# A hybrid mixer trunk on one core: S5's VectorE work is put behind four splits and modulation tiles, and two in-projections move around a norm

## The chip, the cores and the metric

The kernel runs on one core of a Trainium2 chip. The metric is the device time of one execution in microseconds (us). Engines: PE is TensorE's matmul, PEld its weight load, DVE is VectorE, ACT is ScalarE, POOL is GpSimd, and SP is the queue that issues most DMAs. Each engine takes its own instructions strictly in the order in which the program was laid out; between engines there are semaphores.

## The reference, cut to what matters

One layer, 1024 tokens, width 1024, float32:

```python
mod = silu(c) @ w_ada + b_ada                     # 6 x 1024 modulation values
sh1, sc1, g1, sh2, sc2, g2 = split(mod, 6)
h = x * (1 + sc1) + sh1
z = h @ w_in + b_in                               # 14 tiles of 128 columns
z_h, z_b, z_c, z_p, z_cv, z_cg, z_s = split(z, 7)
y_a = z_b * causal_dwconv(z_c * z_h, sc_w)        # short convolution
y_b = pool_mixer(z_p)                             # trailing means
y_c = silu(layer_norm(causal_dwconv(z_cv * sigmoid(z_cg), 31 taps)))   # conformer
y_d = ssm_mixer(z_s)                              # S5: complex diagonal state, then a GLU
y = concat(y_a, y_b, y_c, y_d) @ w_o
x = layer_norm(ALPHA * x + (1 + g1) * y)
x = layer_norm(ALPHA * x + (1 + g2) * ffn(x * (1 + sc2) + sh2))
```

## The kernel before

A float32 matmul is made of three passes (`passes`, L129 to L132) over operands that were cut into a high and a low part. `split` (L80, L81) makes the parts: ACT casts the high one, DVE subtracts to get the low one. `pair` does this for a weight tile of 128x1024 into one of two rotating buffers, `pr0` and `pr1`. Weights come in through `raw` (L73): one SP DMA into one of four rotating 512 KB buffers.

One modulation tile is `ada(j)` (L166): a `raw` load, a DVE multiply with a running sum (L168, 128x1024) and a small DVE add (L170). There are 48.

The order of the stages: a first loop over eight k tiles (L192) does `ada(8+k)`, `ada(k)`, makes `h` for both 512-token halves (ACT L205, splits to `h_a` and `h_b`) and accumulates four of the in-projections (`GRP_A`) in all eight PSUM banks. The last DVE instruction of `ada(7)` is kept as `gate`. Then comes S5's preparation (`SSM.weights`, L1138): a long chain of small operations on 8 to 32 columns, on POOL, from the decay constants to their powers, and from L1216 on operations on 128 and 512 columns on DVE, which multiply those results into four tables; PE transposes them (L1259) and makes kernels (L1270, L1271). Each of those DVE operations is ordered behind `gate`:

```python
i = e.tensor_tensor(out=o, in0=a, in1=b, op=op)
if self.gate is not None and not self.pool:
    self.after(i, self.gate)
```

`SSM.run` (L1302) is the scan itself; its last DMA writes `yg_d` (L1357). The memory of S5 is then given to the pool `yp` (y0 to y7, two more weight pairs `prb`, rows). The first writes into `yp` wait for that last DMA of S5.

Meanwhile PE works through the ten remaining in-projections, `REST` = 11, 9, 4, 0, 5, 1, 6, 7, 2, 3, each one weight pair and two halves (`half`, 24 matmuls each). 11 and 9 feed the conformer's convolution (31 taps on two channel tiles, L429, on DVE). `h_b` is needed up to the last half of projection 3; its memory then takes `ys`, the split operands of the output projection.

The order of DVE, ACT, POOL and SP is laid out by the framework's scheduler from its own costs, by priority of the program's order. In the block from L868 on PE's order is that of the program (`in_order(ON_PE)`). There: the conformer norm's transposes (`run(conf, 2)`: PE L445, DVE statistics L449 and L451, a POOL chain of 14 operations for the reciprocal root, ACT L457), pooling, the two halves of projection 7, then `ada(16)` to `ada(23)`, the norm's second transposes (L463), pooling's matmul (L380), S5's GLU (`ssm_glu`, L294) with the halves of projection 2 between its two parts, projection 3, and the output projection, whose row of gates `g1row` needs `ada(16)` to `ada(23)` and is spread by a DMA of 1024 single values (`spread`, L470).

Of the kernel before, what the change touches and what calls it, by code (L numbers as in the profile page):

```python
# [9 lines left out]
F32 = mybir.dt.float32  # L10
# [4 lines left out]
ADD, SUB, MUL = ALU.add, ALU.subtract, ALU.mult  # L15
# [6 lines left out]
NCH = T // CH  # L22
# [5 lines left out]
TAU = 8  # L28
NS = T // TAU
WARM = 28  # L30
GU_FIRST = 7
CF = 5
T1, T2, T3 = 6, 2, 12
# [3 lines left out]
REST = (11, 9, 4, 0, 5, 1, 6, 7, 2, 3)  # L37
# [13 lines left out]
def trunk(ctx: ExitStack, tc: tile.TileContext, A, out):  # L51
    nc = tc.nc
    V, S, G, PE, SP = nc.vector, nc.scalar, nc.gpsimd, nc.tensor, nc.sync
# [14 lines left out]
    def sm():  # L68
        return ps.tile([P, 512], F32, name="sm", tag="sm", bufs=2)

    def raw(src, cols=1024):
        t = raw_p.tile([P, 1024], F32, name="raw", tag="raw", bufs=4)
        SP.dma_start(t[:, :cols], src)  # L73
        return t
# [3 lines left out]

    def split(hi, lo, src):
        S.copy(hi, src)  # L80
        V.tensor_tensor(out=lo, in0=src, in1=hi.bitcast(F32), op=SUB)  # L81

    def pair(src):
        pt = pair_tile()
        split(pt[:, 0], pt[:, 1], src)
        return pt
# [36 lines left out]
    def run(g, n=1000):  # L123
        for _ in range(n):
            if next(g, g) is g:
                break
# [39 lines left out]
    def ada(j):  # L166
        w = raw(A["w_ada"][j])
        V.scalar_tensor_tensor(out=w, in0=w, scalar=1.0, in1=cond, op0=MUL, op1=MUL,  # L168
                               accum_out=mod[:, j:j + 1])
        return V.tensor_tensor(out=mod[:, j:j + 1], in0=mod[:, j:j + 1], in1=bada[:, j:j + 1], op=ADD)  # L170
# [14 lines left out]
    wm = sm()  # L185
    for i in range(WARM):
        PE.matmul(wm[:, :128], ident, ident, start=True, stop=True)
# [3 lines left out]
            za[m, c] = mm() if m != 10 else sm()  # L191
    for k in range(KT):  # L192
        ada(8 + k)
        gate = ada(k)
        w_k = raw(A["w_inA"][k], 512)
        x_k = tmp()
        step = T if k else CH
        for c0 in range(0, T, step):
            SP.dma_start(x_k[:, c0:c0 + step], A["xT"][k][:, c0:c0 + step])
        wp = pair_tile()  # L200
        split(wp[:, 0, :512], wp[:, 1, :512], w_k[:, :512])
        for c in range(NCH):
            hh, hl = hk(c, k)
            xc = x_k[:, c * CH:(c + 1) * CH]
            S.activation(xc, xc, AF.Identity, scale=mod[:, 8 + k:9 + k], bias=mod[:, k:k + 1])  # L205
            split(hh, hl, xc)
        if k in (0, KT - 1):
            unpack("pack2" if k else "pack1")
        for c in range(NCH):
            for i, m in enumerate(GRP_A):  # L210
                ms = slice(i * P, (i + 1) * P)
                passes(za[m, c], (wp[:, 0, ms], wp[:, 1, ms]), hk(c, k), k == 0, k == KT - 1)
# [20 lines left out]
    def cs(c):  # L233
        return slice(c * CH, (c + 1) * CH)


    def glu_gate(i, zz):
        sg = tmp()
        for c in range(NCH):
            S.activation(sg[:, cs(c)], zz[c], AF.Sigmoid, bias=bin_[:, 10 + i:11 + i])  # L240
        return sg

    def glu_val(i, zz, sg):
        for c in range(NCH):
            V.scalar_tensor_tensor(out=up[i][:, TAPS - 1 + c * CH:TAPS - 1 + (c + 1) * CH], in0=zz[c],
                                   scalar=bin_[:, 8 + i:9 + i], in1=sg[:, cs(c)], op0=ADD, op1=MUL)

    ssm = SSM(tc, A, packs, sp, sm, ident, after)
    scr = {}
# [48 lines left out]
                        in1=sg.rearrange("p (t n) -> p t n", t=TAU), op=MUL)  # L298


    def w_in(m):
        return pair(raw(A["w_inB"][REST.index(m)]))

    def half(w, c):
        o = mm()
        for k in range(KT):
            ks = slice(k * P, (k + 1) * P)
            passes(o, (w[:, 0, ks], w[:, 1, ks]), hk(c, k), k == 0, k == KT - 1)
        return o

    def project(m):
        w = w_in(m)
        return [half(w, c) for c in range(NCH)]

    sg1 = glu_gate(1, project(11))
    glu_val(1, project(9), sg1)

    def short_in(i):
        zc = zch[i][:, 2:]
# [22 lines left out]
    def pool_in(i, c, zz):  # L342
        S.activation(zp[i][:, 16 + c * CH:16 + (c + 1) * CH], zz, AF.Identity, bias=bin_[:, 6 + i:7 + i])
# [4 lines left out]
    for i in range(2):  # L348
        for hf in range(2):
            w = 2 << (2 * i + hf)  # L350
# [35 lines left out]
    zz = project(6)  # L386
# [46 lines left out]
    def conformer(c, acc, bank):  # L433
        nt = tmp()
        st = cst.tile([P, 4, 6], F32, name="cst_", bufs=2)
        mv = cst.tile([P, 4, 2], F32, name="cmv", bufs=2)
        rs = cst.tile([P, 4], F32, name="crs", bufs=2)
        nb = cst.tile([P, 4], F32, name="cnb", bufs=2)
        tp = []
        for h in range(2):  # L440
            o = bank()
            for q in range(2):
                t = 2 * h + q
                for i in range(2):
                    PE.transpose(o[:, q * 256 + i * P:q * 256 + (i + 1) * P],  # L445
                                 acc[i][:, t * P:(t + 1) * P], ident)
            tp.append(o)
        for t in range(4):
            V.bn_stats(st[:, t], tp[t // 2][:, (t % 2) * 256:(t % 2) * 256 + 256])  # L449
        for t in range(4):  # L450
            V.bn_aggr(mv[:, t], st[:, t])  # L451
        rsqrt(rs, mv[:, :, 1])
        G.tensor_tensor(out=nb, in0=mv[:, :, 0], in1=rs, op=MUL)
        G.tensor_scalar(out=nb, in0=nb, scalar1=-1.0, scalar2=None, op0=MUL)
        yield
        for t in range(4):
            S.activation(nt[:, t * 256:(t + 1) * 256], tp[t // 2][:, (t % 2) * 256:(t % 2) * 256 + 256],  # L457
                         AF.Identity, scale=rs[:, t:t + 1], bias=nb[:, t:t + 1])
        yield
        for i in range(2):  # L460
            o = bank()
            for t in range(4):
                PE.transpose(o[:, t * P:(t + 1) * P], nt[:, t * 256 + i * P:t * 256 + (i + 1) * P], ident)  # L463
            S.activation(y[4 + i][:, cs(c)], o, AF.Silu, scale=cfg[:, i:i + 1], bias=cfb[:, i:i + 1])
# [402 lines left out]
    cnt[0] = 2  # L867
    with in_order(ON_PE):  # L868
        w, w2 = w_in(7), w_in(2)
        conf = conformer(0, acc, mm)  # L870
        run(conf, 2)
        fin0 = pooling(0, 0)
        for c in range(NCH):
            pool_in(1, c, half(w, c))
        w3 = w_in(3)
        for j in range(16, 24):
            ada(j)
        fin1 = pooling(1, 0)
        run(conf)
        fin0()  # L880
        ssm_glu(0)
        zz = [half(w2, 0)]
        ssm_glu(1)
        zz.append(half(w2, 1))
        short_out(0, zz)
        fin1()
        for n in range(2):
            wy.append(out_prep(n, K0[n]))
            ada(32 + n)
        acc, taps = conv(1)  # L890
        zz = [half(w3, c) for c in range(NCH)]
        g1row = spread(mod[:, 16:24], "rowa")
        for j in range(34, 40):
            ada(j)
        run(taps, T1)
        short_out(1, zz)

        for n in range(3):
            if n > 1:
                wy.append(out_prep(n, K0[n]))  # L900
            first_step(n)
            ada(24 + 2 * n)
            ada(25 + 2 * n)
            run(taps, T2)
        for j in range(30, 32):
            ada(j)
        for h in range(2):
            o0[3, h] = sm()
        for n in range(3):
            out_step(o0, wy[n][1], wy[n][0], 3, n == 0, False)  # L910
        wy = [out_prep(n, k) for n, k in zip((3, 4, 0, 1, 2), K1)]

        V.tensor_tensor(out=hA, in0=l1g, in1=mod[:, 32:40], op=MUL)
        V.tensor_tensor(out=hB, in0=l1b, in1=mod[:, 32:40], op=MUL)
        V.tensor_tensor(out=hB, in0=hB, in1=mod[:, 24:32], op=ADD)
        ln = []

        def tail(t, lo=0, hi=5):
            for n in range(lo, hi):
                out_step(o0, wy[n][1], wy[n][0], t, False, n == 4)  # L920

        def stats(t):
            rr.append(res1(0, t, o0))
            ln.append(ln1(0, t, rr[t], h2))
            run(ln[t], 1)
        tail(0)
        tail(1)
        tail(2, 0, 2)
# [44 lines left out]
    with tc.issue_after(ln_end[0]), tc.issue_after(ln_end[1]), in_order(ON_PE):  # L973
        for f in range(2, GU_FIRST):
            run(c11(f))
# [24 lines left out]
        def mid():  # L1000
            run(conf)
            spare = [sl.tile([P, 2, 1024], F32R, name="pr", tag=f"m_{n}") for n in ("up", "zch", "zp")]
            cc.extend([c11(GU_FIRST, spare[:2]), c11(GU_FIRST + 1, (spare[2], None))])
            cc.extend(c11(j) for j in range(GU_FIRST + 2, FT // 2))
            run(cc[0], 1)
# [420 lines left out]
```

## Time and profile before

| | |
|---|---|
| median of 3 runs | 1038.14 us (1037.73 to 1041.8) |
| the profiled execution, own time | 1037.87 us |
| its span, first to last instruction | 1036.1 us |
| mean granted TensorE clock | 0.980 |
| busy in the span | PE 980.8, DVE 737.7, ACT 344.5, POOL 184.4 us |

The span is 1.8 us shorter than the execution's own time. PE is busy 95% of the span, so the places where it waits are what the table cannot show and what has to be looked for along the time axis.

### The profile page before, as it was taken

Reading aid. Unit: us, or ns where it says so; the run is one execution under the profiler, and the core shown is the slowest. Engines: PE = TensorE matmul, PEld = TensorE weight load, DVE = VectorE, ACT = ScalarE, POOL = GpSimd, SP = SyncE. Lnnn points to the kernel's source line nnn. Section 1 sums busy time; section 2 is a strip of 40 time slices with the busy share of each in tenths; the row PEclk is TensorE's granted clock in tenths of the full one; section 3 lists DMA queues with packets and bytes.
Section 4 is the critical chain, followed back from the end, with each engine's and each line's share of the span. In section 5 each row is a group of like instructions: output and inputs, shape, how many; then the busy total and the mean of one; then the engine's idle time right before and its main releaser. Section 6 shows DMA issues by size and latency. Waiting matters only on the chain.

```text
span 1036.1 us, 12527 instructions
## 1 busy us (share of the span) xinstructions
PE 980.8 (95%) x4480; PEld 799.9 (77%) x4480; DVE 737.7 (71%) x1184; ACT 344.5 (33%) x537; POOL 184.4 (18%) x515
## 2 busy tenths in 40 slices
PE   8949999898989989899899999999999999999995
PEld 7837777676887868687688888887888888888884
DVE  5858998888669952757898777776568433776656
ACT  4632211424464351374322222222233333312500
POOL 7990000300351020541000000000000000050013
PEclk9979999998999999899999999999999999999998
DMA  8833212686454363597954344443247534654601
GB/s 314 321 112 104 53 41 90 219 225 223 158 204 172 147 237 104 188 316 267 347 175 159 138 147 152 146 148 111 82 149 284 174 136 142 232 185 148 228 21 61
DMA packets 65694, 177.75 MB, mean 172 GB/s; under 512 B 11040, under 2 KB 17216, under 8 KB 65632
## 3 DMA queue, kind: packets, MB, share of 16 engines
q1 hardware_dynamic: 57760, 149.17, 42.7%
q0 software_dynamic: 7872, 27.79, 6.7%
q8 instruction: 35, 0.57, 0.2%
q14 instruction: 27, 0.22, 0.1%
HBM read 142.26 MB, written 34.09 MB: 170 GB/s over the span
## 4 chain that ended last, share of the span: by engine, by line
PE 60%; DVE 10%; DMA 5%; POOL 4%; ACT 3%; issue 2%; SPq 0%; DVEq 0%; POOLq 0%; ACTq 0%
PE mm L132 18%; PE mm L130 18%; PE mm L131 17%; PE sm L130 2%; PE sm L132 2%; PE sm L131 2%; DMA raw<-in_w_ada_dram 2%; DMA raw<-h_d 2%; DVE pr L81 1%; DVE acc L429 1%; DMA raw<-in_w_gate_dram 1%; DVE raw L168 1%; ACT tmp L598 1%; DVE lst L500 1%; POOL rs_a L397 1%
## 5 line engine op out<-in xcount | busy, mean ns | idle before, releaser
L81 DVE TENSOR_TENSOR pr<-raw,pr 128x1024 fp32r<-128x1024 f32 (+1 forms) x139 | 138.1, 1003 | 77.7 <-ACT pr L80 77.4
L80 ACT CAST pr<-raw 128x1024 fp32r<-128x1024 f32 (+1 forms) x139 | 119.2, 878 | 179.4 <-PE sm L132 68.4
L130 PE MATMUL mm<-bop,pr 128*128 128x512 f32 x264 | 103.2, 391 | 4.2 <-DVE c L767 3.5
L131 PE MATMUL mm<-bop,pr 128*128 128x512 f32 x264 | 102.8, 389 | 0.0
L132 PE MATMUL mm<-bop,pr 128*128 128x512 f32 x264 | 102.7, 389 | 0.0
L130 PE MATMUL mm<-h,pr 128*128 128x512 f32 (+1 forms) x208 | 77.0, 370 | 8.0 <-ACT p L643 7.1
L429 DVE SCALAR_TENSOR_TENSOR acc<-up,pack,acc 128x512 f32<-128x512 f32 x120 | 84.3, 742 | 0.1
L130 PE MATMUL mm<-pr,acts 128*128 128x512 f32 x216 | 84.0, 389 | 0.0
L131 PE MATMUL mm<-pr,acts 128*128 128x512 f32 x216 | 84.0, 389 | 0.0
L132 PE MATMUL mm<-pr,acts 128*128 128x512 f32 x216 | 84.0, 389 | 0.0
L132 PE MATMUL mm<-h,pr 128*128 128x512 f32 (+1 forms) x208 | 75.4, 362 | 2.9 <-DVE pr L81 2.9
L131 PE MATMUL mm<-h,pr 128*128 128x512 f32 (+1 forms) x208 | 75.2, 361 | 0.0
L132 PE MATMUL mm<-tb,pr 128*128 128x512 f32 x176 | 68.8, 391 | 1.1 <-DVE pr L81 1.0
L130 PE MATMUL mm<-tb,pr 128*128 128x512 f32 x176 | 68.7, 390 | 1.0 <-ACT pr L80 1.0
L131 PE MATMUL mm<-tb,pr 128*128 128x512 f32 x176 | 68.5, 389 | 0.0
L397 POOL TENSOR_SCALAR rs_a<-lmv 128x1 f32<-128x1 f32 x16 | 11.0, 689 | 318.1 <-DVE lmv L503 317.8
L168 DVE SCALAR_TENSOR_TENSOR raw<-raw,cond 128x1024 f32<-128x1024 f32 x48 | 58.1, 1218 | 13.3 <-DMA raw<-in_w_ada_dram 13.2
L80 ACT CAST pr<-room 128x512 fp32r<-128x512 f32 x60 | 34.3, 619 | 87.9 <-PE mm L132 83.9
L130 PEld LDWEIGHTS mm<-bop,pr 128*128 128x128 f32 x264 | 49.6, 188 | 16.4 <-DVE c L767 2.9
L132 PEld LDWEIGHTS mm<-bop,pr 128*128 128x128 f32 x264 | 49.6, 188 | 10.3
L131 PEld LDWEIGHTS mm<-bop,pr 128*128 128x128 f32 x264 | 49.6, 188 | 10.1
L131 PE MATMUL mm<-h_a,pr 128*128 128x512 f32 x104 | 42.7, 410 | 13.7 <-DVE h_a L81 13.5
(311 smaller groups left out, 2182.4 us busy)
## 6 DMA issues: line engine op xcount, KB each, us to landing
raw<-in_w_ada_dram SPq DMA_DIRECT2D x48, 512.0 KB, 4.8
raw<-in_w_down_dram SPq DMA_DIRECT2D x44, 512.0 KB, 3.7
raw<-in_w_gate_dram SPq DMA_DIRECT2D x23, 512.0 KB, 4.7
raw<-in_w_up_dram SPq DMA_DIRECT2D x23, 512.0 KB, 4.2
raw<-act_d SPq DMA_DIRECT2D x44, 256.0 KB, 3.3
raw<-in_w_o_dram SPq DMA_DIRECT2D x16, 512.0 KB, 4.4
p_d<-p POOLq DMA_DIRECT2D x11, 512.0 KB, 2.9
act_d<-tmp POOLq DMA_DIRECT2D x11, 512.0 KB, 2.9
```

The lines of the kernel that those rows point to most:

```text
L80: S.copy(hi, src)
L81: V.tensor_tensor(out=lo, in0=src, in1=hi.bitcast(F32), op=SUB)
L130: PE.matmul(o, wh, xh, start=first, stop=False, skip_group_check=True)
L131: PE.matmul(o, wh, xl, start=False, stop=False, skip_group_check=True)
L132: PE.matmul(o, wl, xh, start=False, stop=last, skip_group_check=True)
L168: V.scalar_tensor_tensor(out=w, in0=w, scalar=1.0, in1=cond, op0=MUL, op1=MUL, accum_out=mod[:, j:j + 1])
L397: G.tensor_scalar(out=a, in0=v, scalar1=EPS, scalar2=None, op0=ADD)
L429: V.scalar_tensor_tensor(out=o, in0=u, scalar=dww[:, i, j:j + 1], in1=o, op0=MUL, op1=ADD)
L500: V.bn_stats(st[:, h], r[:, h * 512:(h + 1) * 512])
L598: S.activation(dst, src, AF.Identity, scale=hA[:, kk:kk + 1], bias=hB[:, kk:kk + 1])
```

## The change

`w_in` and the pairs of projections 11 and 9 are traced before S5's preparation, and so are `ada(16)` to `ada(19)`; `gate` becomes the last DVE instruction of `ada(19)`. In the later block the halves of projection 7 come before the norm's first transposes, `ada(20)` to `ada(23)` alone are left there, and both halves of projection 2 come between the norm's two sets of transposes. (`split` now returns its instruction; nothing uses it.)

```diff
+EARLY = 4
...
     for k in range(KT):
         ada(8 + k)
-        gate = ada(k)
+        ada(k)
...
+    def w_in(m):
+        return pair(raw(A["w_inB"][REST.index(m)]))
+    w_first = [w_in(m) for m in REST[:2]]
+    for j in range(16, 16 + EARLY):
+        gate = ada(j)
+
     ssm = SSM(tc, A, packs, sp, sm, ident, after)
...
-    def project(m):
-        w = w_in(m)
+    def project(m, w=None):
+        w = w or w_in(m)
         return [half(w, c) for c in range(NCH)]
 
-    sg1 = glu_gate(1, project(11))
-    glu_val(1, project(9), sg1)
+    sg1 = glu_gate(1, project(11, w_first[0]))
+    glu_val(1, project(9, w_first[1]), sg1)
...
     with in_order(ON_PE):
         w, w2 = w_in(7), w_in(2)
+        for c in range(NCH):
+            pool_in(1, c, half(w, c))
         conf = conformer(0, acc, mm)
         run(conf, 2)
         fin0 = pooling(0, 0)
-        for c in range(NCH):
-            pool_in(1, c, half(w, c))
         w3 = w_in(3)
-        for j in range(16, 24):
+        for j in range(16 + EARLY, 24):
             ada(j)
         fin1 = pooling(1, 0)
+        zz = [half(w2, c) for c in range(NCH)]
         run(conf)
         fin0()
         ssm_glu(0)
-        zz = [half(w2, 0)]
         ssm_glu(1)
-        zz.append(half(w2, 1))
         short_out(0, zz)
```

## Rows read from the trace of the kernel before

**Rows 1.** What PE waited for, by releaser: total us, times, longest us.

```profile
PE mm L131 <- DVE h_a L81: 13.5, 2, 13.1
```

**Rows 2.** PE's timeline, 52 to 74: start, us, what, [idle before <- releaser].

```profile
52.10 0.39 PE L130 MATMUL mm<-h_b,pr 128*128 128x512 f32 x1
...
53.46 0.39 PE L130 MATMUL mm<-h_a,pr 128*128 128x512 f32 x1
66.91 0.79 PE L131 MATMUL mm<-h_a,pr 128*128 128x512 f32 x1 [13.06 <-DVE h_a L81]
...
74.00 0.63 PE L1259 MATMUL sm<-ident,w 128*128 128x128 f32 x4
```

**Rows 3.** DVE's timeline from 48.

```profile
48.04 1.21 DVE L168 SCALAR_TENSOR_TENSOR raw<-raw,cond 128x1024 f32<-128x1024 f32 x1
...
60.21 0.58 DVE L1089 TENSOR_TENSOR s<-pack,s 128x128 f32<-128x128 f32 x2 [10.14 <-POOL s L1089]
...
65.56 0.69 DVE L1089 TENSOR_TENSOR t<-pack,s 128x512 f32<-128x512 f32 x1 [1.23 <-POOL s L1089]
66.17 0.68 DVE L81 TENSOR_TENSOR h_a<-tmp,h_a 128x512 fp32r<-128x512 f32 x1
...
92.42 1.23 DVE L81 TENSOR_TENSOR pr<-raw,pr 128x1024 fp32r<-128x1024 f32 x1 [1.47 <-ACT pr L80]
...
142.47 8.70 DVE L429 SCALAR_TENSOR_TENSOR acc<-up,pack,acc 128x512 f32<-128x512 f32 x13
```

**Rows 4.** Stretches: PE, PEld, DVE, ACT, POOL busy (x instructions), clock, DMA.

```profile
30.00:40.00 10.00, 10.00 (x46) 8.29 (x45) 8.76 (x19) 6.55 (x11) 9.23 (x18) 1.00 0.96 372
40.00:50.00 10.00, 10.00 (x46) 8.29 (x45) 8.20 (x18) 5.03 (x9) 9.20 (x19) 1.00 0.83 287
...
50.20:65.60 15.40, 3.65 (x17) 2.68 (x15) 1.57 (x5) 1.85 (x4) 15.28 (x87) 0.71 0.37 136
...
188.30:199.20 10.90, 9.00 (x40) 7.13 (x38) 9.66 (x21) 0.03 (x1) 9.68 (x14) 1.00 0.74 266
```

**Rows 5.** DMA issues, 0 to 110: size and median us to landing.

```profile
raw<-in_w_inB_dram SPq DMA_DIRECT2D x8, 512.0 KB, 4.8
```

**Rows 6.** SP's timeline, 40 to 110.

```profile
49.06 24.54 SPq L73 DMA_DIRECT2D raw<-in_w_inB_dram  x5
```

**Rows 7.** Where S5 ends: timelines of DVE, ACT and PE, 174 to 186.

```profile
178.74 0.88 DVE L332 TENSOR_SCALAR y<-zch,pack 128x512 f32<-128x512 f32 x2 [1.30 <-DMA yg_d<-st]
...
180.71 1.99 ACT L80 CAST pr<-raw 128x1024 fp32r<-128x1024 f32 x2
...
181.78 2.36 DVE L81 TENSOR_TENSOR pr<-raw,pr 128x1024 fp32r<-128x1024 f32 x2 [1.49 <-ACT pr L80]
...
185.37 1.03 PE L445 MATMUL mm<-ident,acc 128*128 128x128 f32 x8
```

**Rows 8.** The conformer norm: timelines of POOL and PE, 188 to 203.

```profile
188.38 1.12 POOL L397 TENSOR_SCALAR rs_a<-cmv 128x4 f32<-128x4 f32 x1 [60.90 <-DVE cmv L451]
...
198.91 0.23 POOL L454 TENSOR_SCALAR cnb<-cnb 128x4 f32<-128x4 f32 x1
...
199.79 2.70 PE L463 MATMUL mm<-ident,tmp 128*128 128x128 f32 x8 [2.49 <-ACT tmp L457]
```

**Rows 9.** DMA issues, 199 to 216.

```profile
raw<-in_w_ada_dram SPq DMA_DIRECT2D x4, 512.0 KB, 11.3
rowa_d<-mod SPq DMA_DIRECT2D x1, 4.0 KB, 9.5
```

**Rows 10.** Into the output projection: timelines of PE and ACT, 231 to 240.

```profile
233.15 0.39 PE L132 MATMUL mm<-h_b,pr 128*128 128x512 f32 x1
236.44 0.50 PE L130 MATMUL mm<-pr,ys 128*128 128x512 f32 x1 [2.91 <-ACT ys L80]
...
238.46 0.79 PE L132 MATMUL mm<-pr,ys 128*128 128x512 f32 x1 [1.28 <-DVE ys L81]
...
234.83 1.04 ACT L80 CAST pr<-raw 128x1024 fp32r<-128x1024 f32 x1 [11.49 <-DMA raw<-in_w_o_dram]
```

More of the change, by code (lines that the diff above doesn't have):

```diff
@@ L80, in split @@
         S.copy(hi, src)
-        V.tensor_tensor(out=lo, in0=src, in1=hi.bitcast(F32), op=SUB)
+        return V.tensor_tensor(out=lo, in0=src, in1=hi.bitcast(F32), op=SUB)
     def pair(src):
@@ L298, in ssm_glu @@
                         in1=sg.rearrange("p (t n) -> p t n", t=TAU), op=MUL)
-    def w_in(m):
-        return pair(raw(A["w_inB"][REST.index(m)]))
     def half(w, c):
```

## The prediction, as put on record before the result

> **What bounds the kernel now.** I read the page first, then PE's waits, then the timelines around the longest of them. PE is busy for 980.8 of 1036.1 us, so only its idle places can give much. The longest single wait is 13.1 us [rows 1]. PE's timeline shows where: in the first loop's last k tile PE does one matmul at 53.46 and the next at 66.91, released by DVE's split of `h_a` [rows 2]. DVE is not busy then. It stands for 10.14 us in front of an S5 operation that waits for POOL, goes on at 60.21, waits again, and splits `h_a` only at 66.17 [rows 3]. So `h_a` was ready on ACT, but queued on DVE behind S5, and S5 behind POOL. The stretch table shows why POOL takes just until then: 37 POOL instructions in 30 to 50 with DVE busy for 16.96 us, 87 in the 15.4 us to 65.6 with DVE busy for 1.57 [rows 4]. POOL runs freely only because DVE stands still.
>
> The end of S5 matters too. DVE's first write into `yp` waits for S5's last DMA until 178.74; ACT casts projection 7's pair at 180.71, DVE splits it at 181.78, and PE is through with projection 6 at 185.37 [rows 7]. PE thus reaches projection 7 only some 2 us after its pair exists. Whatever PE wins earlier, it can spend only as far as S5 ends earlier.
>
> **The change, part one: the gate.** What the 13 us give back. With the gate behind `ada(19)`, DVE can split `h_a` as soon as ACT delivers it. PE then goes on without a break: the starts from 52.10 to 53.46 are 0.227 apart [rows 2], the 24 matmuls end at 58.9, and projection 11 with its 48 matmuls (10.9 us) can follow, for its pair is now made early. The slow restart (the first matmul after the wait takes 0.79 instead of 0.39) I leave in, since PE will wait again.
>
> When the gate opens. Today five `w_inB` loads are queued from 49.06, and four fill the four `raw` buffers [rows 6]. Now these four are the weights of 11 and 9 and tiles 16 and 17. A load lands after 4.8 us [rows 5], so at 54 to 57; tiles 18 and 19 need buffers that DVE frees at about 57, land at 62, and the gate opens at about 64. That alone would cost nothing: POOL's results come at 60.21 to 65.56 anyway. Past SP's other work the moved loads cost nothing: today SP stands in front of the fifth load until 73.6 [rows 6] and nothing behind it is missed. What is queued on DVE behind S5's first waiting operation is the GLU value, the taps and the pair of projection 4; PE needs that pair only after projections 11 and 9, at 80 or later.
>
> What it costs POOL. DVE now works in the stretch in which it stood: two `h` splits (0.68 each, 1.3 together) and four tiles of 1.21 [rows 3], two pairs in 2.36 [rows 7], 8.5 us. What this does to POOL is read from rows 4: 15.4 us over 87 is 0.177 us for one instruction with DVE nearly still; at that rate 37 instructions are 6.5 us, but they took 20, so 13.5 us were lost over 16.96 us of DVE work, 0.80 of it. Bounds: 0 and 8.5 us; I take 0.80, measured twenty microseconds earlier on the same chain, so 6.8 us. POOL's last result comes at 72.4 instead of 65.56.
>
> The Trainium skill ("SBUF — State Buffer", section "Who interferes with whom") says that a VectorE instruction with two inputs in SBUF and a GpSimd instruction that reads SBUF exclude each other for the whole instruction. This rule speaks against the change; by it POOL would lose all 8.5 us and the sum below would be 1.7 us higher. The rows are milder, since POOL gets about one instruction in between two of DVE's, and I go by them.
>
> S5 after that. The two `h` splits (1.3) no longer stand inside its work, nor does the first pair (1.2), in whose place the scheduler will put one convolution tap (13 taps in 8.70, so 0.67) [rows 3]. PE's first S5 transposes move from 74.00 [rows 2] by 6.8 - 1.3 - 1.2 + 0.7 = +5.0, to 79.0. By then projection 11 is done, so PE is ahead by 10.9 - 5.0 = 5.9 us: the stall has moved behind projection 11 and shrunk. The rest of S5 loses the second pair to a tap (-0.5) and DVE's 1.47 us wait at 92.42 for a pair buffer [rows 3], which PE now frees earlier. S5's last DMA lands at 178.74 + 5.0 - 0.5 - 1.5 = 181.7. From there one cast (1.0) and one split (1.2) lead to projection 7 at about 184.0. PE arrives at 185.37 - 5.9 = 179.5 and waits. Its gain is the smaller of the two, 185.37 - 184.0 = **1.4 us**. Bounds: if POOL loses nothing, 8.2 us; if it loses all, nothing.
>
> **Part two: the norm.** Today transposes start at 185.37 [rows 7]; POOL's 14 operations run from 188.38 to 199.1, 10.8 us, while DVE is busy for 9.66 of 10.9 [rows 4, 8]. The halves of projection 7 (10.9) cover it but for 2.49 us, and the transposes after that wait take 2.70 instead of 1.03 [rows 7, 8]. In the new order projection 2's halves give the same cover, so the wait stays unless POOL's chain falls to 10.8 - 2.5 = 8.3 us. Fourteen instructions at 0.177 are 2.5 us; four tiles fewer take 4.8 us of DVE's work away, which leaves 2.5 + 0.8 x 4.9 = 6.4. I take the wait as gone: -(2.49 + 1.67) = -4.2. The second GLU part now follows the first without a half between them and waits for ACT to empty its two PSUM banks; two ACT passes of 1024 columns take 1.99 [rows 7], these have 512 each, so between 0 and 2: +1.0. Together **-3.2**; bounds -4.2 and +2.
>
> **Part three: into the output projection.** After projection 3 (last matmul at 233.15) PE gets going at 238.46 [rows 10]. ACT's `ys` casts stand behind a cast that waited 11.49 us for a `w_o` load [rows 10], which queued behind modulation tiles; those took 11.3 us each while the 4 KB spread of the gate row took 9.5 [rows 9]. That chain loses four loads and 4.8 us of DVE. PE comes 4.6 us earlier, so the gap stays as it is if the chain gains just that (0), and shrinks to one cast and one split of 512 columns, about 1.4, if it gains more (-3.9). I take the middle, **-1.9**.
>
> The tiles and pairs themselves are only moved, and PE's matmuls are the same ones. Behind 240 everything shifts along. Sum: 1037.87 (own time; span 1036.1) - 1.4 - 3.2 - 1.9 = **1031.4**; the median of the runs stands 0.3 above this execution.
>
> **The rivals.** *POOL is not held up.* If the tiles arrive in pieces that leave POOL its time, S5 ends 6.8 us earlier and part one gives 8.2: 1024.6. For it: 1.57 us of DVE work lay in POOL's free stretch without harm. Against it: rows 4 in 30 to 50. *The stall only moves.* Projection 7 waits for S5, POOL's chain still takes 10.8 us because DVE fills the freed time with other tiles, and the `w_o` load stays late: 1.4 less the 1.0 for the GLU, 1037. For it: DVE is the one that fills 188 to 199 today. *Slower.* Convolution taps are ready before S5 begins, since `glu_val(0)` no longer waits; the scheduler may put one in each of S5's dependency gaps. Each delays S5 by 0.67 and POOL by another 0.5. From the 1.4 of part one the loss is one for one; with parts two and three at nothing it takes some six taps to pass 5 us: 1043. Against it: taps that run now are gone later.
>
> **How the numbers follow.** A run of this kernel can tell about 0.5% (5 us) from no change. Forecast 0.50 (1027 to 1035.5), POOL free 0.17, stall moves 0.20, slower 0.13. Of the forecast's half, three quarters lie beyond 5 us; with POOL free that is 0.56 faster. Same: the rest of the forecast, the moved stall and some of the taps, 0.34. Slower: 0.10. The range reaches from 1022, a little past POOL free, to 1040, which leaves out the worst of the taps.
>
> **What would show it.** PE without a wait at 53.9, and a wait of 6 to 11 us in front of L1259 instead; POOL's last S5 results near 72, not 65; S5's last DMA near 181; projection 7 following it at once; a norm chain on POOL of 8 us or less; the wait before L463 gone. The prediction is wrong if S5 ends well before 178, or after 185, or if DVE still stands before `h_a`.

## The result and the profile after

The changed kernel took 1047.44 us (median of 13 runs, 1040.89 to 1052.33), the kernel before 1039.14 us beside it (13 runs, 1036.5 to 1041.8): a ratio of 1.0077, 95% interval 1.0056 to 1.0097. The profiled execution took 1046.63 us over a span of 1044.9, so the span is 8.8 us longer. Forecast were 1031.4 us and a range of 1022 to 1040; the time lies above it, on the side that had 0.10. Line numbers of the changed kernel are one to eight higher (L1259 is now L1263, L463 is L468, L1353 is L1357).

PE's waits from 40 to 300 (waited for, us in total, times, longest), to be read against [rows 1]:

```profile
PE sm L1263 <- DVE w L1093: 7.1, 1, 7.1
PE mm L131 <- ACT pr L81: 6.0, 1, 6.0
PE mm L468 <- ACT tmp L462: 5.1, 1, 5.1
PE sm L1357 <- DVE st L1093: 3.7, 2, 2.6
PE mm L133 <- DVE pr L82: 2.5, 2, 2.0
```

The wait of 13.1 us before `h_a` is gone. In its place PE waits for S5 three times (first transposes, last matmuls, projection 7's pair), 16.8 us in all, and the norm's wait has doubled from 2.49 to 5.1. The windows show where, and at which clock (columns as in [rows 4]):

```profile
60.00:70.00 10.00, 10.00 (x46) 8.29 (x45) 5.58 (x13) 3.00 (x5) 10.00 (x40) 1.00 0.99 330
70.00:80.00 10.00, 3.67 (x17) 2.70 (x15) 8.23 (x17) 1.49 (x2) 9.59 (x29) 0.95 0.27 111
80.00:90.00 10.00, 9.26 (x49) 7.10 (x50) 9.45 (x16) 1.17 (x2) 3.62 (x6) 0.71 0.16 54
...
170.00:180.00 10.00, 6.26 (x25) 4.56 (x24) 8.96 (x15) 1.62 (x2) 0.00 (x0) 0.73 0.13 49
180.00:190.00 10.00, 7.95 (x29) 5.87 (x27) 2.79 (x6) 1.08 (x2) 0.00 (x0) 0.50 0.17 56
190.00:200.00 10.00, 5.63 (x15) 4.07 (x16) 7.17 (x11) 3.05 (x3) 0.00 (x0) 0.58 0.99 336
```

In 180 to 190 PE is busy for 7.95 us at a granted clock of 0.50, the lower of its two levels. The kernel before has 1.00 in every window from 100 to 200. Six rows of DVE's timeline tell S5's course, against [rows 3, 7]:

```profile
51.25 0.69 DVE L82 TENSOR_TENSOR h_a<-tmp,h_a 128x512 fp32r<-128x512 f32 x1 [1.50 <-ACT h_a L81]
...
72.73 0.69 DVE L1093 TENSOR_TENSOR t<-pack,s 128x512 f32<-128x512 f32 x1 [1.24 <-POOL s L1093]
...
84.88 0.75 DVE L246 SCALAR_TENSOR_TENSOR up<-mm,pack,tmp 128x512 f32<-128x512 f32 x1 [0.56 <-PE mm L133]
...
95.38 0.75 DVE L246 SCALAR_TENSOR_TENSOR up<-mm,pack,tmp 128x512 f32<-128x512 f32 x1 [2.50 <-PE mm L133]
...
100.92 0.25 DVE L1093 TENSOR_TENSOR t<-tab 128x8 f32<-128x8 f32 x2
...
192.83 0.88 DVE L337 TENSOR_SCALAR y<-zch,pack 128x512 f32<-128x512 f32 x2 [8.44 <-DMA yg_d<-st]
```

POOL's last result (the last time DVE waits for POOL inside S5's preparation) comes at 72.73 instead of 65.56 (+7.2), S5's table (tile `tab`) starts at 100.92 instead of 90.70 (+10.2), the last `st` (what S5's last matmuls read) at 175.18 instead of 166.40 (+8.8), and the first write into S5's old memory at 192.83 instead of 178.74 (+14.1). The last step is made on PE (its timeline):

```profile
172.79 0.49 PE L1357 MATMUL sm<-st,VR 64*128 64x127 f32 x4 [1.10 <-DVE st L1093]
175.92 0.79 PE L1357 MATMUL sm<-st,VI 64*128 64x127 f32 x2 [2.64 <-DVE st L1093]
...
187.32 0.63 PE L1357 MATMUL sm<-st,VI 64*128 64x127 f32 x2
193.93 0.77 PE L131 MATMUL mm<-h_a,pr 128*128 128x512 f32 x1 [5.98 <-ACT pr L81]
```

From 175.92 on, S5's last matmuls take 12.0 us; the same ones took 6.8 before (167.37 to 174.12), with projection 6 ahead of and behind them (PE's timeline of the kernel before):

```profile
167.37 0.48 PE L1353 MATMUL sm<-st,VI 64*128 64x127 f32 x2
...
174.12 0.50 PE L132 MATMUL mm<-h_b,pr 128*128 128x512 f32 x1
```

In the changed kernel projection 6 ends at 171.7, and PE has nothing else: projection 7's pair lies in S5's memory. Then the norm, from the timelines of PE, DVE and POOL, against [rows 8]:

```profile
207.50 1.03 PE L450 MATMUL mm<-ident,acc 128*128 128x128 f32 x8
...
208.09 1.23 DVE L169 SCALAR_TENSOR_TENSOR raw<-raw,cond 128x1024 f32<-128x1024 f32 x1 [5.18 <-DMA raw<-in_w_ada_dram]
...
209.79 1.23 DVE L169 SCALAR_TENSOR_TENSOR raw<-raw,cond 128x1024 f32<-128x1024 f32 x1 [0.27 <-DMA raw<-in_w_ada_dram]
...
211.13 1.42 DVE L454 BATCH_NORM_STATS2 cst__1796<-mm 128x6 f32<-128x256 f32 x4
...
212.92 1.12 POOL L402 TENSOR_SCALAR rs_a<-cmv 128x4 f32<-128x4 f32 x1 [76.27 <-DVE cmv L456]
...
222.70 1.16 POOL L459 TENSOR_SCALAR cnb<-cnb 128x4 f32<-128x4 f32 x1
...
224.51 2.69 PE L468 MATMUL mm<-ident,tmp 128*128 128x128 f32 x8 [5.08 <-ACT tmp L462]
```

The statistics stand on DVE behind two modulation tiles whose loads, issued from 199.68 on, land only at 208 and 209.8; just ahead of them, at 198.55, SP issued the 4 KB spread of the gate row, which took 10.8 us here [rows 9]. So the statistics start 3.6 us after the transposes, where they took 1.2 before, and POOL's 14 operations take 10.9 us, as before. The output projection starts at 247.61 instead of 236.44 (+11.2).

### The profile page after: what moved, and what is told of

It reads as the page before. It is cut to its first block, busy times and chain, and to the rows that moved or that the text cites. A ratio compares the mean times of both kernels' runs of the same rounds, so it can differ in the third digit from the quotient of the medians.

```text
span 1044.9 us, 12527 instructions
## 1 busy us (share of the span) xinstructions
PE 987.6 (95%) x4480; PEld 804.6 (77%) x4480; DVE 737.7 (71%) x1184; ACT 344.2 (33%) x537; POOL 190.7 (18%) x515
## 4 chain that ended last, share of the span: by engine, by line
PE 56%; DVE 11%; POOL 5%; issue 5%; DMA 4%; ACT 2%; DVEq 0%; SPq 0%; POOLq 0%; ACTq 0%
PE mm L131 16%; PE mm L133 16%; PE mm L132 16%; PE sm L131 2%; PE sm L132 2%; PE sm L133 2%; DVE pr L82 2%; DVE acc L434 2%; DMA raw<-h_d 1%; DMA room<-in_w_gate_dram 1%; DMA raw<-in_w_ada_dram 1%; ACT tmp L603 1%; DVE lst L505 1%; POOL rs_a L402 1%; DVE raw L169 1%
## 5 line engine op out<-in xcount | busy, mean ns | idle before, releaser
L132 PE MATMUL mm<-h,pr 128*128 128x512 f32 (+1 forms) x208 | 75.7, 364 | 0.0
L131 PEld LDWEIGHTS mm<-h,pr 128*128 128x128 f32 x208 | 40.4, 194 | 15.0 <-ACT p L648 7.7
```

Source lines behind the costliest of these rows:

```text
L131: PE.matmul(o, wh, xh, start=first, stop=False, skip_group_check=True)
L132: PE.matmul(o, wh, xl, start=False, stop=False, skip_group_check=True)
```

## The experiments

Beside the ratio, three places serve as marks: S5's last DMA issue, the first matmul of the output projection, and a wait of 3.9 to 4.2 us that PE has in every version before the same matmul of the feed-forward (L130 <- ACT `p`, at 433.29 before), by which all of this work is done. The marks are read from one execution each. From the mark to the end of the span the versions differ by up to 8 us (602.3 to 610.5) although no edit touches that part, so what a mark gains need not show in the time. "Out" is the output projection's first matmul; PE can wait again right behind it (8.1 us in version 1). "Before" is the kernel before, run on the same chip.

| version | us | before | ratio, 95% | POOL's last | S5's DMA | out | mark |
|---|---|---|---|---|---|---|---|
| before | | | | 65.56 | 175.38 | 236.44 | 433.29 |
| changed | 1047.44 | 1039.14 | 1.0077, 1.0056 to 1.0097 | 72.73 | 189.15 | 247.61 | 442.59 |
| changed, again | 1053.24 | 1043.5 | 1.0102, 1.0081 to 1.0123 | 73.10 | 187.71 | 248.32 | 443.52 |
| 1 gate alone | 1059.0 | 1043.91 | 1.0158, 1.012 to 1.0197 | 73.40 | 188.15 | 243.75 | 447.89 |
| 2 order alone | 1040.0 | 1043.91 | 0.9961, 0.9941 to 0.9982 | 66.19 | 176.25 | 232.08 | 431.56 |
| 3 gate on the h split | 1039.49 | 1043.91 | 0.9952, 0.9931 to 0.9973 | 66.91 | 178.35 | 230.92 | 429.43 |
| 4 early pair | 1040.25 | 1043.91 | 0.997, 0.995 to 0.999 | 73.47 | 188.07 | 235.59 | 431.49 |
| 5 PE filled | 1049.97 | 1043.68 | 1.0063, 1.0042 to 1.0083 | 72.39 | 183.18 | 242.99 | 439.30 |
| 6 late GLU | 1049.52 | 1043.68 | 1.0063, 1.0039 to 1.0088 | 73.14 | 189.96 | 248.82 | 443.86 |
| 7 no tiles | 1039.31 | 1043.5 | 0.9956, 0.9935 to 0.9977 | 69.24 | 180.27 | 236.03 | 431.62 |
| 8 no tiles, early pair | 1038.52 | 1043.68 | 0.995, 0.9934 to 0.9967 | 70.20 | 180.78 | 230.54 | 431.64 |
| 9 order, early pair | 1040.24 | 1043.68 | 0.9962, 0.9942 to 0.9982 | 65.23 | 175.08 | 236.95 | 433.40 |
| 10 as 8, late taps | 1032.72 | 1040.08 | 0.9923, 0.9905 to 0.9942 | 67.95 | 174.03 | 228.41 | 428.87 |
| 11 as 9, late taps | 1037.22 | 1040.08 | 0.9975, 0.9955 to 0.9995 | 66.18 | 172.94 | 235.80 | 431.58 |

**1 and 2: each part alone.** Version 1 has the early pairs, tiles and gate, and the old order behind S5; version 2 has the old gate and the new order with all eight tiles.

```diff
 # 2: on the kernel before
+        for c in range(NCH):
+            pool_in(1, c, half(w, c))
         conf = conformer(0, acc, mm)
         run(conf, 2)
         fin0 = pooling(0, 0)
-        for c in range(NCH):
-            pool_in(1, c, half(w, c))
...
+        zz = [half(w2, c) for c in range(NCH)]
         run(conf)
```

> Part one of the change alone: the gate behind tile 19 and the first two pairs early; the later block in the order of before, with four tiles left in it. Theory one (S5's chain, delayed by 7 us on POOL and 3 us by what stands in its gaps, and its last matmuls at half the clock because PE has run out of projections, carries the loss): the loss is nearly all here, S5's last transfer lands near 192, TensorE's clock falls to 0.5 in 180 to 190, and the time lies 5 to 10 us above before. Rival (the reordered norm block carries it): no more than 2 us above before, and S5's late end is paid back there.

> Part two alone: the gate and S5 as before, projection 7's halves in front of the norm's transposes and projection 2's behind, all eight tiles in the later block. Theory one: S5's last transfer lands at 178 to 179 as before, and the time is within 4 us of before, since the norm's cover is one projection either way. Rival: 5 to 10 us above before, with a wait of 5 us or more before the norm's second transposes although S5 ends as early as before.

The gate part carries the loss (+1.6%, more than expected); the reordered block alone gains 0.4%. In the old order the late S5 costs even more, because the norm's part on ACT then stands ahead of projection 7's casts, and waits for POOL (ACT's timeline of version 1):

```profile
196.45 1.02 ACT L462 ACTIVATE tmp<-mm,cnb,crs 128x256 f32<-128x256 f32 x2 [8.32 <-POOL cnb L459]
197.36 1.99 ACT L81 CAST pr<-raw 128x1024 fp32r<-128x1024 f32 x2
```

In version 2 the norm went as forecast: POOL's chain takes 7.8 us, and the wait before the second transposes is gone (POOL's timeline).

```profile
199.53 1.12 POOL L397 TENSOR_SCALAR rs_a<-cmv 128x4 f32<-128x4 f32 x1 [71.21 <-DVE cmv L451]
...
207.06 0.23 POOL L454 TENSOR_SCALAR cnb<-cnb 128x4 f32<-128x4 f32 x1
```

**3 and 7: how much of DVE's work stands in POOL's stretch.** Version 3 puts the gate behind the last split of `h` and leaves nothing else there; version 7 keeps the two pairs, takes the second one's DVE split as the gate (`w_in_gate` gives back both), and drops only the tiles (their work and their four loads go back to the later block).

```diff
 # 3
-EARLY = 4
+EARLY = 0
-            split(hh, hl, xc)
+            gate = split(hh, hl, xc)
 # 7
-EARLY = 4
+EARLY = 0
-    w_first = [w_in(m) for m in REST[:2]]
+    w_first = [w_in(REST[0])]
+    pt, gate = w_in_gate(REST[1])
+    w_first.append(pt)
```

> The changed kernel with the gate behind the last split of h instead of tile 19, and tiles 16 to 19 back in the later block. PE's 13 us wait should be gone as in the changed kernel, without four tiles of 1.2 us and their loads in POOL's stretch. Theory one: POOL's last results come 3 to 5 us earlier than in the changed kernel (68 to 70 instead of 72.7), S5 ends by as much earlier or a little more, TensorE's low clock at S5's end shrinks or goes, and the time lies 3 to 8 us below the changed kernel. Rival (POOL's slowing is not what counts): within 2 us of the changed kernel.

> The changed kernel without tiles 16 to 19 ahead of S5: the gate stands behind the split of projection 9's pair, and all eight tiles lie in the later block. The pair buffer of projection 7 is as in the changed kernel. This takes 4.8 us of DVE's work out of POOL's stretch and nothing else. Theory one: POOL's last result comes 16 to 17 us after h_a's split instead of 20 to 21.5, S5 ends 5 to 9 us earlier than in the changed kernel (the lower figure if its last matmuls still run at half clock), and the time lies 5 to 9 us below the changed kernel. Rival (projection 7's wait for S5's memory carries the whole loss, whenever S5 ends): within 3 us of the changed kernel.

> The changed kernel itself, unedited, beside the version without the four early tiles, so that the two are compared on one chip. Both theories: some 0.8% above before, as measured.

Four tiles, 4.9 us of DVE's work with their loads, make the whole difference between 1.0102 and 0.9956 on one chip: 13.9 us between the medians, 13.2 between the spans, more than theory one had. From `h_a`'s split to POOL's last result it is 21.2 us with them (51.86 to 73.10), 16.5 without (52.72 to 69.24) and 15.1 in version 3 (51.83 to 66.91). The changed kernel is behind version 7 by 3.9 us at POOL's last result and 3.0 at the last `st` (174.53, 171.49), but by 7.4 at S5's last DMA, for in version 7 S5's last matmuls run at full clock (172.25 to 179.1, 6.8 us). At the norm's second transposes it is 13.1 (224.24, 211.15), for version 7 has no wait there and the other one of 6.3 us. Projection 7 waits 5.9 us for S5's memory in version 7 too, so the rival falls. Version 3 shows what the 13 us before `h_a` were worth: with that wait gone, PE waits 9.83 us for projection 11's pair, queued on DVE behind S5 (PE's timeline), and the time is that of version 2, which still has the wait.

```profile
69.80 0.79 PE L133 MATMUL mm<-h_a,pr 128*128 128x512 f32 x1 [9.83 <-DVE pr L82]
```

**5: PE's clock.** 28 matmuls that feed nothing, behind projection 6.

```diff
+    warm_o = mm()
+    for i in range(28):
+        PE.matmul(warm_o, h_a[:, 0, 0, :P], h_a[:, 0, 0], start=i == 0, stop=i == 27, ...)
```

> The changed kernel with 28 more matmuls of 512 columns on PE (of h_a with itself into a bank that nobody reads), written behind projection 6; 16 of them stand ahead of S5's last matmuls and 12 behind. They are no part of what is computed. They do nothing for the order of the other work; they only keep PE from standing still where it has run out of projections. Theory one with the clock as a term of its own: the granted clock stays at 1.00 in 170 to 190, S5's 72 last matmuls take about 7 us instead of 12, S5's last transfer lands some 5 us earlier, projection 7's first matmuls run at 0.227 too, and the time falls by 4 to 8 us below the changed kernel although PE has 6.4 us more work. Rival (the clock is only a sign of the wait and costs nothing by itself): the same time as the changed kernel or up to 6 us more.

The windows of version 5:

```profile
170.00:180.00 10.00, 9.80 (x53) 7.21 (x52) 7.97 (x13) 1.62 (x2) 0.00 (x0) 1.00 0.20 61
180.00:190.00 10.00, 5.73 (x27) 4.00 (x26) 5.62 (x11) 3.08 (x4) 0.00 (x0) 1.00 0.71 234
```

The clock stays at 1.00, the last matmuls take 6.8 us (175.16 to 181.97) instead of 12.0, and S5's last DMA leaves 6.0 us earlier; 1.0 of that is there at the last `st` already (174.18), 5.0 come after it. So the clock is a cost of its own at S5's end. Projection 7's first matmuls fell to the lower clock all the same, which theory one had not: after waits of 3.33 and 0.93 us they start 0.43 apart from 190.39 to 193.38. Of the 6.0 us the mark shows 3.3, in part since the norm's wait grows from 5.1 to 6.3. The gain in time that theory one forecast is not shown: the ratio, 1.0063, lies below both of the changed kernel, 1.0077 and 1.0102, but its interval overlaps both, and version 6 has the same ratio without the filling.

**4, 8 and 9: projection 7 without S5's memory.** One digit: the pair rotation starts at 1, so projection 7 takes the buffer that projection 1 frees. 4 does it to the changed kernel, 8 to version 7, 9 to version 2.

```diff
     pairs.append((yp, "prb", 2))
-    cnt[0] = 2
+    cnt[0] = 1
```

> The changed kernel with projection 7's weights in a pair buffer that projection 1 frees, instead of one that takes S5's memory. Nothing else is edited. Theory one (PE has run out of projections and waits for S5's memory): projection 7 no longer waits for S5's last transfer at 192.7 but starts by 188 or before, and the time falls by 5 to 12 us below the changed kernel, below before too if S5's last matmuls run at full clock. Rival (the loss lies in the norm block and behind it): within 2 us of the changed kernel, the wait only moves behind projection 7.

> The gate behind the split of projection 9's pair, no modulation tiles ahead of S5 (all eight in the later block, in the changed order), and projection 7's weights in the pair buffer that projection 1 frees. PE's 13 us wait is gone, POOL is slowed by two splits of h and two pairs only. Theory one (what PE gains is worth something if S5 ends not much later than before and projection 7 need not wait for it): POOL's last results at 68 to 70, S5's last transfer by 185, no clock below 0.9 in 160 to 190, and 6 to 12 us below before. Rival (another chain sets the end once the first two waits are gone): not more than 3 us below the version with the gate on the h split (which was 0.5% below before).

> The kernel before with the changed order of the later block and projection 7's weights in the pair buffer that projection 1 frees; the gate as before, so PE still stands for 13 us before h_a. Theory one (an early pair is worth something only if PE comes to projection 7 before S5 ends): within 2 us of the reordered block alone (0.4% below before). Rival (the pair is worth 10 us wherever it is, as in the changed kernel): 8 to 12 us below before.

In the changed kernel the digit takes away the wait before projection 7 and 11.1 us at the mark: the wait for S5's memory was real. S5 itself ends as late in version 4 as in the changed kernel (188.07), and its last matmuls run at the lower clock (0.50 in 180 to 190); the expectation had tied a time below before to full clock, and the time came out below before all the same. In version 9 the digit does nothing for the ratio, as expected, since PE comes to projection 7 no earlier than S5 ends. In version 8 the rival holds: the output projection starts 5.5 us earlier than in version 7, but at the mark nothing is left (431.64 against 431.62). The lead melts on the way: from 5.5 us to 2.2 a hundred matmuls later (259.86 against 262.04), 1.3 at 356 and nothing at 383. What takes it in each of these stretches stays open. At S5's end the clock of version 8 is 1.00, as expected.

**6, 10 and 11: what stands in S5's gaps.** 6 orders the second GLU value behind S5's weights; 10 and 11 order there the convolution's first tap, on both channel tiles, of the first 512 tokens; the other taps of these tokens hang on it.

```diff
 # 10, 11: in taps() of conv(c)
-                        V.tensor_scalar(out=o, in0=u, scalar1=dww[:, i, 0:1], ...)
+                        first = V.tensor_scalar(out=o, in0=u, scalar1=dww[:, i, 0:1], ...)
+                        if c == 0:
+                            after(first, ssm.last)
```

> The changed kernel with the two DVE operations of the second GLU value (which wait for projection 9 on PE) ordered behind S5's weights; the taps that hang on them move too. Theory one (DVE waits in order for PE inside S5's weights: 0.56 and 2.50 us, and 1.5 us of the two operations): S5's table begins 2 to 4 us earlier (97 to 99 instead of 100.9), S5 ends as much earlier, and the time falls by 2 to 5 us. Rival (the gaps are filled anyway, and only POOL's late results count): within 1.5 us of the changed kernel.

> The version with the gate behind projection 9's pair and the early pair for projection 7, and with the first tap of each half of the convolution ordered behind S5's last operation on its weights, so that no tap stands in S5's dependency gaps before its table; the same taps are done later. Theory one (S5's chain on DVE carries the time up to projection 7, and each tap in its gaps delays it one for one): S5's table begins 16 to 18 us after POOL's last result instead of 28, S5's last transfer lands at 176 to 179 instead of 184.4, PE's low clock near 80 shrinks, and the time falls by 3 to 8 us below that version. Rival (DVE is full from 70 to 170 either way; what S5 gains the taps lose, and the norm then waits for its taps): S5 ends earlier, but the time is within 2 us of that version, with a wait before the norm's first transposes.

> The kernel before with the reordered later block, the early pair, and the taps behind S5's last operation on its weights; the gate as before. Theory one (S5's chain carries the time only if PE is ahead of it): S5 ends 7 us or more earlier than before, but PE, which stands 13 us before h_a, does not come to projection 7 any earlier, so the time stays within 2 us of the same version with the taps in the gaps (0.4% below before). Rival (S5's end carries the time in every version): 4 to 8 us below it.

Version 6 is a miss for theory one. From POOL's last result to the table it is 28.4 us as in the changed kernel (28.2). DVE no longer waits for the GLU's matmuls but for the next pair, whose buffer the same projection 9 frees (DVE's timeline):

```profile
97.31 1.22 DVE L82 TENSOR_TENSOR pr<-raw,pr 128x1024 fp32r<-128x1024 f32 x1 [3.17 <-ACT pr L81]
...
101.58 0.25 DVE L1095 TENSOR_TENSOR t<-tab 128x8 f32<-128x8 f32 x2
```

So it is not the GLU that is late, but projection 9, after PE's wait of 6.97 us (7.07 in the changed kernel) and at a clock of 0.64 in 80 to 90 (0.71). Version 10 has the lowest ratio, 0.77% below before: S5's last DMA leaves at 174.03, 6.8 us earlier than in version 8, and 2.8 us of that remain at the mark. Of the 6.8 us, 2.3 are there at POOL's last result already. Its table comes 23.0 us after POOL's last result, not 16 to 18, for DVE waits for projection 9 here too (DVE's timeline of version 10):

```profile
88.18 0.75 DVE L246 SCALAR_TENSOR_TENSOR up<-mm,pack,tmp 128x512 f32<-128x512 f32 x1 [3.81 <-PE mm L133]
...
90.97 0.26 DVE L1101 TENSOR_TENSOR t<-tab 128x8 f32<-128x8 f32 x2
```

Against version 8 the gain in the ratio (0.9923 to 0.995) is not shown, for the intervals overlap. Version 11, where PE stands before `h_a`, gains nothing from the same edit, as theory one said; but S5's last DMA leaves only 2.4 us earlier than before there, not 7, so this is the weaker half of the pair.

## Why the prediction was wrong

**Right: the stall and POOL.** PE has no wait at 53.9, and 7.07 us before L1263, within the 6 to 11 forecast. POOL's last result comes at 72.73, forecast 72.4. The prediction went by rows that it called milder than a rule, and its price was close; what the rows hide is that the rule holds. The rule of the Trainium skill ("SBUF — State Buffer", section "Who interferes with whom") that was weighed there has a VectorE instruction with two inputs in SBUF and a reading GpSimd instruction shut each other out. The trace of the changed kernel bears it out. Rows of DVE's and of POOL's timeline:

```profile
54.62 1.22 DVE L82 TENSOR_TENSOR pr<-raw,pr 128x1024 fp32r<-128x1024 f32 x1 [2.08 <-ACT pr L81]
58.70 0.75 DVE L246 SCALAR_TENSOR_TENSOR up<-mm,pack,tmp 128x512 f32<-128x512 f32 x1 [1.47 <-ACT tmp L241]
61.69 1.22 DVE L82 TENSOR_TENSOR pr<-raw,pr 128x1024 fp32r<-128x1024 f32 x1
...
54.74 1.17 POOL L1093 TENSOR_TENSOR s<-s 128x8 f32<-128x8 f32 x1
58.74 0.20 POOL L1093 TENSOR_TENSOR s<-s,s 128x8 f32<-128x8 f32 x1
61.79 1.19 POOL L1093 TENSOR_TENSOR s<-s 128x8 f32<-128x8 f32 x1
```

In the stretch from `h_a`'s split (51.25) to S5's first waiting operation (67.34) DVE has eight large instructions with two inputs in SBUF: two `h` splits, two pairs, four tiles. Under each of them lies one POOL instruction that lasts until DVE's ends, 0.63 to 1.27 us; no other POOL instruction there takes more than 0.3. Beside the GLU value at 58.70, one of whose inputs (`mm`) lies in PSUM, POOL goes on at 0.20. The loads are not what slows POOL: in 57.20 to 59.30, with DMA busy at 0.92, it does 14 instructions in 2.10 us. The windows from `h_a`'s split to S5's first waiting operation, version 3 first, then the changed kernel, give the price:

```profile
51.83:61.56 9.73, 8.13 (x36) 6.39 (x35) 1.29 (x3) 7.91 (x9) 9.73 (x54) 1.00 0.41 144
```

```profile
51.25:67.34 16.09, 16.09 (x72) 13.33 (x72) 10.15 (x18) 9.79 (x11) 16.02 (x55) 1.00 0.84 289
```

POOL does 54 instructions in 9.73 us with the two `h` splits alone beside it (DVE busy for 1.29), and 55 in 16.09 with the pairs and tiles as well: at the first rate 55 take 9.9, so 6.2 us were lost. The pairs and tiles are 7.2 us, so 0.86 of it was lost; forecast 0.80. The rest is the one POOL instruction that gets done under each.

**Wrong: "S5 after that", the step from 79.0 to projection 7 at 184.0.** Three of its figures failed, and they put S5's end and with it projection 7 some 10 us later than forecast.
- Of the savings before L1263 (h splits 1.3, the pair against a tap 0.5) only 0.4 came (8.0 us from POOL's last result instead of 8.4): two taps and the pair of projection 4 stood there. 80.74 instead of 79.0: +1.7.
- The rest of S5 was to lose 2.0 (a tap for a pair, DVE's wait of 1.47). From POOL's last result to the table it took 28.2 instead of 25.1 us. That is 0.56 and 2.50 of waiting, in DVE's order, for a projection that PE now does late. The 1.47 itself did go: from the table to the last `st` it took 74.3 instead of 75.7. Up to the last `st` that is +4.0 against the forecast. The prediction had looked at DVE's queue for work, not for waits that the moved stall would make. The forecast "slower" rival, taps in the gaps, was not the cause: two more taps than before stood there, and two `h` splits fewer.
- PE's lead was thought to be lost as waiting alone. But S5's own last matmuls lie in that hole; at half the clock they took 12.0 us instead of 6.8. This term was in no part of the sum: from the last `st` to S5's last DMA it took 14.0 instead of 9.0, +5.0. Versions 5 and 7 show it: with the hole filled or shortened the clock stays up, and the same stretch takes 9.0 and 8.8 us.

Projection 7 starts at 193.93, not 184.0; PE came to the same block at 185.37 before: the gain of 1.4 became a loss of 8.6. The prediction's own sign of being wrong, S5 ending after 185, is there: the write that waits for its last DMA comes at 192.83. Projection 7's first nine matmuls take 4.7 us, 0.44 of it waiting, instead of 2.0; the clock is 0.50 there.

The loss needs two things together: S5's late end, and projection 7 hanging on it by its buffer. In version 4 S5 ends as late, without the tie, and the ratio is 0.997; in version 7 the tie is left and PE still waits 5.9 us for it, but S5 ends 7.4 us earlier, and the ratio is 0.9956.

**The norm, -3.2 forecast.** Its wait grew by 2.6 and its restart takes 2.69 as before. The mechanism was right, as version 2 shows (POOL's chain 7.8 us, limit 8.3; ratio 0.9961), but it hung on projection 7 coming in time: in version 4, where S5 is late and projection 7 is not, the wait is 0.6. With projection 7 late, the tiles, the spread and their loads fall into the norm's own stretch, DVE is busy for 9.92 of 10 us there (210 to 220), and the chain stays at 10.9.

**Into the output projection, -1.9 forecast.** The two waits of 2.91 and 1.28 [rows 10] have become 0.95: -3.2, within the bounds. That PE comes 11 us later is not all of it: in version 4, also with four tiles there, PE comes at 235.59 and the waits are 1.1. Together: 11.2 us late at the output projection, 9.3 at the mark, 8.8 at the end.

**The frame.** That PE's 13.1 us were worth little while S5 ends no earlier was in the prediction and holds: versions 2, 3, 7 and 8, with and without that wait, lie between 0.995 and 0.9961. What part one lacked was a loss side; the "slower" rival had one, by another mechanism (taps). Bounding part one by "nothing" if POOL loses all assumed that S5 late by a few microseconds is late by just those. Four tiles of 1.22 us cost 14. One sum of the chances is off a little: three quarters of 0.50 and 0.17 are 0.545, not 0.56.

## What to carry to other kernels

A wait on the busiest engine is worth what the chain behind it allows: find the chain that ends last in the stage, and price every instruction that the edit puts beside or into it, waits in issue order included. When the edit makes the engine run out of work ahead of that chain, look for the chain's own instructions on that engine, for they may run at the lower clock, as here. If such a hole must be, a buffer that lets the next independent work start (one digit here, 1.3% against the changed kernel run again, each by its own before) is worth more than keeping the clock up in it (11.1 us at the mark in version 4, 3.3 in version 5).

## What was not expected of the hardware

PE's granted clock fell at S5's end: in the changed kernel after a wait of 1.10 us and four small matmuls, within a wait of 2.64 (1.00 in 173.28 to 174.00, 0.50 in 175.00 to 175.90), before S5's last matmuls began. Version 4, with waits of 0.65 and 2.64 in these places, went to the lower level too, a little over 1 us after its last matmuls had begun (1.00 in 175.83 to 177.00, 0.55 in 177 to 178), while version 5, with twelve matmuls of 512 columns in place of the second wait, stayed at 1.00. The Trainium skill ("TensorE: Matmul & The Clock Gate", Part 1, "The HAM clock gate") says that the throttled state is the default and activity releases it; the traces agree (0.50 in 180 to 190 of the changed kernel, 1.00 there in version 5). And PE carried 6.4 us of useless work in version 5 at no cost that could be measured. A POOL instruction of 0.2 us under a DVE instruction with two inputs in SBUF lasted until that one ended, to 0.1 us, in all eight cases of the stretch read above.
